# Fresh weight sums on VectorE for one pair of each gate quarter, and a fifth seven-product pair in the first

## The chip, the cores and the metric

The kernel runs on one core of a Trainium2 chip, in one launch. The metric is the device time of that launch in microseconds. All matrix products run on TensorE (PE); VectorE (DVE), ScalarE (ACT) and GpSimd (POOL) prepare operands and finish results; the queues of SyncE (SP), ScalarE and POOL start transfers, which share the core's 16 DMA engines.

## The reference

One encoder block, 256 tokens of width 2048, float32. What matters here is the middle of it, the two gates and what they multiply:

```python
h = rms_norm(x, attn_norm[i])
proj = h @ w_in[i]
qa, ka, va, qb, kb, vb, ga, gb = jnp.split(proj, split_points, axis=-1)
ya = windowed_gqa(qa, ka, va, rel_bias_table, sink_a[i])
yb = dilated_attention(qb, kb, vb, rel_bias_table)
merged = jax.nn.sigmoid(ga) * (ya @ w_branch_a[i]) + jax.nn.sigmoid(gb) * (yb @ w_branch_b[i])
x = x + merged @ w_out[i]
...
x = x + (jax.nn.gelu(g) * (hf @ w_ffn_up[i])) @ w_ffn_down[i]
gate_p = jax.nn.sigmoid(rms_norm(x, ple_norm[i]) @ w_ple_gate[i])
x = x + gate_p * (p[i] @ w_ple_proj[i])
```

`ga` and `gb` are each 2048 columns of `w_in`: 256 x 2048 by 2048 x 4096 in all.

## The kernel before

All weights lie in memory as one stream of pieces, 16 blocks of 128 x 128 each, in the order of use (`_stream`). A load brings half a piece (8 blocks, 512 KB) into one of six `raw` buffers. Every product is made to float32 accuracy from two parts: ScalarE copies the weights, rounded, to `whi` (L287), VectorE puts the rest, `raw - whi`, into `wlo` (L288), and three matmuls (`xhi*whi`, `xhi*wlo`, `xlo*whi`, L474 to L476) make one product. There are four `whi` and four `wlo` buffers, so a split can be at most four steps ahead of TensorE; a matmul of 512 columns follows the one before as soon as its operands are there.

The gates are made in four quarters (jobs `gab` 0 to 3). A quarter covers 4 blocks of columns of each gate and all 16 blocks of the inner dimension, taken as 8 pairs. Between the quarters stand the branch products (`ba`, `bb`, 8 and 4 blocks of the inner dimension). `seven_product` (L451) works a pair as a 2 x 2 by 2 x 2 block product, over the two inner blocks, the two halves of the tokens and the two gates: 8 products, or 7 by combining sums of operands as Strassen and Winograd do, after which VectorE and ScalarE combine the accumulators (`combined`). Which pairs take seven, and in which order the pairs come, is in `_pairs` (L141): in a quarter the order is 0, 4, 1, 2, 6, 3, 5, 7, and pairs 1, 2, 3 and 5 (`GATED`) take seven.

A pair by eight has two splits of 128 x 1024 and 24 matmuls. A pair by seven has four parts, with 3, 6, 6 and 6 matmuls, and `split_to` (L275) writes this order for VectorE: the `wlo` of part 0 (128 x 512); an add that makes the sum `t2` (L296); the `wlo` of part 1, the *sums* tile (128 x 1024); an add that makes `t4` (L298); the `wlo` of part 2 and of part 3, which reads both sums. `keep` holds this order fast. The sums tile of part 1 has two sums of weight blocks, b11 + b12 and b12 + b22. These are made ahead in memory: `sums_in_memory` (L327) has POOL copy two blocks within memory and add the others to them by accumulating transfers, at the places listed in `MADE_AT`, for the first `AHEAD` = 29 seven-pairs (5 of the values job `v8`, 16 of the gates, 8 of the output projection); later ones are made in another way (`quarters`). `back` (L351) loads the finished tile on SP's queue into one of two buffers, two pairs ahead.

The operand sums of the activations for a seven-pair (`of_input`) are made once, before. The first job that uses them, `v8`, takes five pairs by seven, 1, 2, 3, 5 and 6 (`FARS`, `of_first`); the sums for pair 6 lie in the tile `first`.

```python
GATED = (1, 2, 3, 5)
...
    if kind == "gab":
        return [0, 4, 1, 2, 6, 3, 5, 7], GATED
...
            if part == 0 and not _whole(a):
                keep(nc.vector.tensor_tensor(t2, raws[h][:, :4, :], pairs_of[a][:, :4, :], op=ALU.add))
            if part == 1:
                keep(nc.vector.tensor_tensor(t4, raws[h][:, 4:, :], t2, op=ALU.add))
```

Of the kernel before, what the change touches and what calls it, by code (L numbers as in the profile page):

```python
# [13 lines left out]
ALU = mybir.AluOpType  # L14
AX = mybir.AxisListType

P = 128
# [19 lines left out]
PIECE = 16  # L37
SUB = 8
# [21 lines left out]
def _plan():  # L60
# [48 lines left out]
    for half in range(2):  # L109
# [7 lines left out]
        for c in range(2):  # L117
# [5 lines left out]


TOGETHER = 3
AHEAD = 8 + 5 + 4 * 4
SAVED = 8
SPLIT = 4
ROWS = 7
# [3 lines left out]
GATED = (1, 2, 3, 5)  # L133
# [1 line left out]
FETCHED = ((24, 8), (28, 8), (32, 8), (36, 8), (38, 9), (38, 14), (49, 8), (49, 12))  # L135
MADE_AT = [(9, 1), (10, 8), (11, 14), (13, 4), (14, 12), (16, 14), (18, 2),
           (19, 4), (19, 9), (19, 14), (20, 8), (21, 3), (23, 8), (25, 8), (27, 12), (30, 0), (31, 14),
           (34, 0), (37, 0), (38, 4), (38, 11), (39, 2), (40, 6), (40, 12), (41, 3), (43, 4), (43, 11), (44, 5), (46, 0)]


def _pairs(kind, c):  # L141

    if kind == "pgs":
        return [0, 1, 4, 5, 2, 6, 7, 3], range(4, 8)
    if kind == "v8":
        return [0, 1, 2, 4, 3, 5, 6, 7], FARS
    if kind == "gab":
        return [0, 4, 1, 2, 6, 3, 5, 7], GATED
    if kind == "o":
        return ([2, 4, 5, 6, 7, 0, 1, 3] if c else [0, 1, 2, 4, 5, 6, 7, 3]), range(LATER, LATER + 4)  # L150
    if kind == "d1" and c == 1:
        return [5, 0, 1, 6, 2, 3, 7, 4, 8, 9, 10], range(5)
    return [8, 0, 1, 2, 3, 9, 4, 5, 6, 7, 10], range(SAVED)
# [32 lines left out]
_SEVEN, _EIGHT, _ENDS = [], set(), {}  # L186
# [5 lines left out]
def _whole(a):  # L192

    if _BLOCKS[a][0] == "w_in":
        return False
    return _BLOCKS[a][0] in ("w_out", "w_ple_gate") or (_BLOCKS[a + SUB][1] % FHALF) // 2 in WHOLE
# [19 lines left out]
def _encoder(ctx: ExitStack, tc, xt, pt, cols, table, onehot, mask, ident_in, last_gain, wts, xrows, out):  # L216
    nc = tc.nc
# [31 lines left out]
    keep = tc.keep_in_program_order  # L249


    raws, subs = {}, {}
    pairs_of, kept = {}, {}
# [21 lines left out]
    def split_to(i):  # L275
        while state["sub"] < min(i, len(_SUBS)):
            s = state["sub"]
            a, n, part = _SUBS[s]
            h, o = divmod(a, SUB)
            load_all(h + 6 + (part == 3))  # L280
            if part is None:
                src = raws[h][:, o:min(o + n, SUB), :]
            else:
                src = (raws[h + 1][:, :4, :], pairs_of.get(a), raws[h], raws[h + 1])[part]
            hi = wpool.tile(list(src.shape), FR, name="whi", bufs=4)
            lo = wpool.tile(list(src.shape), FR, name="wlo", bufs=4)
            nc.scalar.activation(hi, src, AF.Copy)  # L287
            ins = nc.vector.tensor_tensor(lo, src, hi.bitcast(F32), op=ALU.subtract)  # L288
            if a // PIECE * PIECE in _EIGHT:
                keep(ins)  # L290
            subs[s] = (hi, lo)
            state["sub"] = s + 1
            if part is not None:
                t2, t4 = raws[h + 1][:, 4:, :], raws[h + 1][:, :4, :]
            if part == 0 and not _whole(a):
                keep(nc.vector.tensor_tensor(t2, raws[h][:, :4, :], pairs_of[a][:, :4, :], op=ALU.add))  # L296
            if part == 1:
                keep(nc.vector.tensor_tensor(t4, raws[h][:, 4:, :], t2, op=ALU.add))  # L298
                j = _SEVEN.index(a)
                if all(not j <= e < j + (3 if j > _ENDS["gab"] else 2) for e in _LAST):  # L300
                    back()
# [49 lines left out]
    def back():  # L351

        j = state["back"]
        t = two_sums() if "ff" in held else ap_.tile([P, SUB, P], F32, name="sums", tag="near", bufs=2)
        pairs_of[_SEVEN[j]] = t
        nc.sync.dma_start(t, kept[j][0])
        state["back"] = j + 1

    def firsts_to(end):
# [226 lines left out]
    def at(i, f, *a):  # L586

        due.setdefault(i, []).append((f, a))
# [78 lines left out]
    b = ps.tile([NH, 2 * T], F32, name="misc")  # L667
# [232 lines left out]
    def of_input(m):  # L900
        e = SPLIT + 2 * GATED.index(m)
        return [shared[:, e + c, :].rearrange("p (b n) -> p b n", n=P) for c in range(2)]

    def of_first(m):
        if m in (2, 3, 5):
            return of_input(m)
        return [held["first"][:, 2 * (m == 6) + c, :].rearrange("p (b n) -> p b n", n=P) for c in range(2)]
# [215 lines left out]
    def fetch(t, c):  # L1123
# [8 lines left out]
    stills = {  # L1132
        "o": lambda k: held["merged"][k >= SPLIT][:, k - SPLIT * (k >= SPLIT), :], "ba": lambda k: yab[:, k, :],
        "bb": lambda k: yab[:, QH + k, :], "pp": lambda k: held["ps"][:, k, :], "pg": lambda k: held["pl"][:, k, :],
    }
    stills["v"] = movers["q"]

    for i, job in enumerate(_JOBS):
        kind, n, _, _, _, blocks = job
# [23 lines left out]

        for e, (j, k) in enumerate(MADE_AT):
            if j == i:
                at((j, k), sums_in_memory, e)
        if i == _FAR - 6:
            held["first"] = big.tile([P, SPLIT, 2 * T], FR, name="first", tag="b0", bufs=1)
            for j, m in ((0, 1), (1, 5), (2, 6), (4, 2), (5, 3)):
# [13 lines left out]
        if kind == "gg" or (kind == "g" and n == FHALF):  # L1183
            late = 3 * (kind == "g")
            for e in range(16 if kind == "gg" else 17):
                j = i + late + (9 * e // 4 if late else 5 * e // 2)
# [58 lines left out]
        elif kind in ("o", "d0", "d1", "gab", "pgs", "v8"):  # L1245
# [2 lines left out]
            tags = {a: b for e in range(2) for a, b in zip(names[e], places[e ^ {"gab": n != 3, "v8": 0}.get(kind, n)])}  # L1248
            if (kind, n) == ("gab", 0):
                tags.update(p3="sp", p4="sp", c22="acc", p1="acc", p6="pt", p7="pt", p5="misc")  # L1250
            still, sums_at = {"o": (stills["o"], early), "gab": (stills["v"], of_input), "pgs": (stills["pg"], of_residual),
                               "v8": (stills["v"], of_first)}.get(
                kind, (lambda k: held["act"][:, k, :], shl))
            if kind == "v8":
# [134 lines left out]
```

## Time and profile before

| | us |
|---|---|
| median of three runs | 1443.81 (1443.23 to 1443.97) |
| the profiled execution | 1444.3 |
| its span, first to last instruction | 1442.5 |
| first gate quarter (`gab` 0) on TensorE | 312.9 to 356.3 |
| second, third, fourth | 361.7 to 403.5, 419.8 to 461.5, 461.5 to 502.3 |
| granted TensorE clock, mean | 0.998 |

A row of the timeline gives the start in us, how long the instructions took in us, the engine, the line, the operation, output <- inputs by the program's names, sizes and a count; in brackets stands the idle time of the engine ahead of it, and what ended that. Neighbours of one kind are merged into a row (x2), which then runs from the first one's start to the last one's end; on VectorE and ScalarE an instruction starts a little before the last one's end. Matmuls overlap: the spacing of their starts is what one costs, not the length shown.

### The profile page before, as it was taken

Reading aid. Unit: us, or ns where it says so; the run is one execution under the profiler, and the core shown is the slowest. Engines: PE = TensorE matmul, PEld = TensorE weight load, DVE = VectorE, ACT = ScalarE, POOL = GpSimd, SP = SyncE. Lnnn points to the kernel's source line nnn. Section 1 sums busy time; section 2 is a strip of 40 time slices with the busy share of each in tenths; the row PEclk is TensorE's granted clock in tenths of the full one; section 3 lists DMA queues with packets and bytes.
Section 4 is the critical chain, followed back from the end, with each engine's and each line's share of the span. In section 5 each row is a group of like instructions: output and inputs, shape, how many; then the busy total and the mean of one; then the engine's idle time right before and its main releaser. Section 6 shows DMA issues by size and latency. Waiting matters only on the chain.

```text
span 1442.5 us, 21000 instructions
## 1 busy us (share of the span) xinstructions
PE 1431.2 (99%) x7452; PEld 1227.1 (85%) x7452; DVE 1183.9 (82%) x1635; ACT 876.3 (61%) x1256; POOL 188.3 (13%) x291
## 2 busy tenths in 40 slices
PE   9999999999999999999999999999999999999997
PEld 8898888888888888888888888888888888888886
DVE  7798966668879878878888878997888887998896
ACT  7576654456656656775555556776555555677864
POOL 0022222111222110201111100102111110010000
PEclk9999999999999999999999999999999999999999
DMA  9798998889999978968888887989988888799672
GB/s 327 252 244 255 301 292 247 253 231 295 293 295 320 279 238 301 300 220 301 301 287 296 288 300 243 266 292 299 310 307 303 314 302 295 250 294 285 211 240 93
DMA packets 128149, 397.31 MB, mean 275 GB/s; under 512 B 14628, under 2 KB 19876, under 8 KB 127916
## 3 DMA queue, kind: packets, MB, share of 16 engines
q1 hardware_dynamic: 93372, 300.79, 60.4%
q0 software_dynamic: 32656, 91.24, 24.4%
q10 hardware_dynamic: 2016, 3.94, 0.9%
q8 instruction: 58, 0.95, 0.3%
q14 instruction: 47, 0.39, 0.1%
HBM read 363.11 MB, written 58.76 MB: 292 GB/s over the span
## 4 chain that ended last, share of the span: by engine, by line
PE 95%; DVE 2%; DMA 1%; ACT 1%; issue 0%; SPq 0%; POOLq 0%; DVEq 0%; ACTq 0%
PE acc L395 29%; PE acc L398 15%; PE acc L475 12%; PE acc L476 12%; PE acc L474 12%; PE acc L423 3%; PE acc L425 3%; PE acc L424 3%; PE first L372 2%; DMA raw<-in_wts 1%; DVE wlo L288 1%; PE pt L987 1%; PE pt L754 1%; PE acc L447 0%; ACT whi L287 0%
## 5 line engine op out<-in xcount | busy, mean ns | idle before, releaser
L288 DVE TENSOR_TENSOR wlo<-raw,whi 128x1024 fp32r<-128x1024 f32 (+2 forms) x581 | 660.8, 1158 | 94.9 <-ACT whi L287 87.2
L287 ACT ACTIVATE whi<-raw 128x1024 fp32r<-128x1024 f32 (+2 forms) x581 | 573.5, 1005 | 234.6 <-PE acc L476 92.0
L395 PE MATMUL acc<-mov,whi 128*128 128x512 f32 x1840 | 441.3, 391 | 0.0
L395 PEld LDWEIGHTS acc<-mov,whi 128*128 128x128 f32 x1840 | 337.8, 188 | 65.5
L398 PEld LDWEIGHTS acc<-mov,wlo 128*128 128x128 f32 x1840 | 237.3, 191 | 9.0 <-ACT mov L531 0.2
L398 PE MATMUL acc<-mov,wlo 128*128 128x256 f32 x1840 | 243.1, 283 | 0.0
L512 ACT ACTIVATE t<-acc 128x256 f32<-128x256 f32 x115 | 43.6, 379 | 149.6 <-PE acc L395 149.6
L476 PE MATMUL acc<-whi,mov 128*128 128x512 f32 x259 | 100.8, 389 | 0.0
L475 PE MATMUL acc<-wlo,mov 128*128 128x512 f32 x259 | 100.8, 389 | 0.0
L474 PE MATMUL acc<-whi,mov 128*128 128x512 f32 x259 | 100.6, 390 | 0.0
L288 DVE TENSOR_TENSOR wlo<-sums,whi 128x1024 fp32r<-128x1024 f32 x62 | 75.5, 1219 | 8.9 <-ACT whi L287 8.9
L474 PE MATMUL acc<-whi,act 128*128 128x512 f32 x207 | 80.9, 391 | 0.0
L475 PE MATMUL acc<-wlo,act 128*128 128x512 f32 x207 | 80.7, 390 | 0.0
L476 PE MATMUL acc<-whi,act 128*128 128x512 f32 x207 | 80.7, 390 | 0.0
L287 ACT ACTIVATE whi<-sums 128x1024 fp32r<-128x1024 f32 x62 | 65.4, 1056 | 20.4 <-PE acc L476 9.4
L934 POOL DMA_DIRECT2D x<-row x33 | 28.5, 908 | 310.8 <-PE acc L476 106.0
L325 POOL DMA_DIRECT2D kept<-sums x33 | 17.8, 540 | 360.2 <-DVE sums L321 219.4
L475 PE MATMUL acc<-wlo,merged 128*128 128x512 f32 x164 | 64.1, 391 | 0.3 <-DVE wlo L288 0.2
L474 PE MATMUL acc<-whi,merged 128*128 128x512 f32 x164 | 64.0, 390 | 0.0
L476 PE MATMUL acc<-whi,merged 128*128 128x512 f32 x164 | 63.9, 389 | 0.0
L857 ACT ACTIVATE c<-c 128x256 f32<-128x256 f32 x44 | 18.3, 417 | 67.2 <-DVE c L855 67.2
L476 PEld LDWEIGHTS acc<-whi,mov 128*128 128x128 f32 x259 | 48.6, 188 | 10.1
(274 smaller groups left out, 2147.9 us busy)
## 6 DMA issues: line engine op xcount, KB each, us to landing
raw<-in_wts SPq DMA_DIRECT2D x452, 512.0 KB, 6.0
sums<-kept SPq DMA_DIRECT2D x62, 512.0 KB, 5.8
kept<-in_wts POOLq DMA_DIRECT2D x66, 256.0 KB, 8.0
sums<-in_wts POOLq DMA_DIRECT2D x33, 512.0 KB, 7.3
kept<-sums POOLq DMA_DIRECT2D x33, 512.0 KB, 4.6
raw<-in_wts SPq DMA_DIRECT2D x64, 256.0 KB, 5.2
kept<-in_wts POOLq DMA_DIRECT2D x29, 512.0 KB, 7.7
x<-row POOLq DMA_DIRECT2D x33, 256.0 KB, 7.9
```

The source lines that it names most:

```text
L287: nc.scalar.activation(hi, src, AF.Copy)
L288: ins = nc.vector.tensor_tensor(lo, src, hi.bitcast(F32), op=ALU.subtract)
L372: nc.tensor.matmul(firsts[e][:, T * low:], w, m[:, :2 * T - T * low], start=(k == 0 and not low), stop=(k == KC - 1 and low != turned), sk ...
L395: nc.tensor.matmul(acc, hi[:, k, :], m, start=(first and k == 0), stop=(last and k == SUB - 1), skip_group_check=True)
L398: nc.tensor.matmul(acc[:, T:], lo[:, k, :], m[:, :T], start=False, stop=False, skip_group_check=True)
L423: nc.tensor.matmul(acc, xh, hi, start=(k == 0), stop=False)
L424: nc.tensor.matmul(acc, xh, lo, start=False, stop=False)
L425: nc.tensor.matmul(acc, xl, hi, start=False, stop=(k == n - 1 - t * late))
L474: nc.tensor.matmul(acc, xh, hi, start=(e == 1), stop=False)
L475: nc.tensor.matmul(acc, xh, lo, start=False, stop=False)
L476: nc.tensor.matmul(acc, xl, hi, start=False, stop=(e == uses[name]))
L512: keep(nc.scalar.activation(t, acc[:, T:], AF.Copy, scale=scale))
```

## The change

For one pair of each quarter, number 8, 13, 17 and 21 in the list of all seven-pairs (`FRESH`), the sums of weights aren't made in memory. `back` loads the two blocks as they are, b11 and b12, and VectorE makes both sums in place where they are used, by two adds of 128 x 512 behind the `wlo` of part 0. Number 8 is pair 6 of the first quarter, which took eight products before and now takes seven, with the operand sums in `first`; the order there becomes 0, 4, 1, 2, 3, 6, 5, 7. Numbers 13, 17 and 21 are pair 5, the last seven-pair, of the other quarters. `sums_in_memory` is run for 26 pairs instead of 29, and `MADE_AT` moves the last ones.

```diff
 TOGETHER = 3
-AHEAD = 8 + 5 + 4 * 4
+AHEAD = 5 + 5 + 3 * 4 + 8
...
-           (34, 0), (37, 0), (38, 4), (38, 11), (39, 2), (40, 6), (40, 12), (41, 3), (43, 4), (43, 11), (44, 5), (46, 0)]
+           (34, 0), (36, 8), (37, 6), (38, 5), (38, 12), (41, 3), (43, 6), (45, 2), (46, 2)]
+FRESH = (8, 13, 17, 21)
+KEPT = [j for j in range(AHEAD) if j not in FRESH]
...
+    if kind == "gab" and c == 0:
+        return [0, 4, 1, 2, 3, 6, 5, 7], (*GATED, 6)
     if kind == "gab":
         return [0, 4, 1, 2, 6, 3, 5, 7], GATED
...
+            if part == 0 and _SEVEN.index(a) in FRESH:
+                two, b22 = pairs_of[a], raws[h][:, :4, :]
+                for dst, more in ((two[:, :4, :], two[:, 4:, :]), (two[:, 4:, :], b22)):
+                    keep(nc.vector.tensor_tensor(dst, dst, more, op=ALU.add))
             if part == 0 and not _whole(a):
...
-        nc.sync.dma_start(t, kept[j][0])
+        nc.sync.dma_start(t, wts[_SEVEN[j] // PIECE].rearrange("p (b n) -> p b n", n=P)[:, SUB:, :] if j in FRESH else kept[j][0])
...
+    def of_gated(m):
+        return of_first(m) if m == 6 else of_input(m)
...
-                at((j, k), sums_in_memory, e)
+                at((j, k), sums_in_memory, KEPT[e])
...
-            still, sums_at = {"o": (stills["o"], early), "gab": (stills["v"], of_input), "pgs": (stills["pg"], of_residual),
+            still, sums_at = {"o": (stills["o"], early), "gab": (stills["v"], of_gated), "pgs": (stills["pg"], of_residual),
```

VectorE's queue at the last seven-pair of the second quarter (pair 5). Before, from part 0 to part 3 and the first split of pair 7; `raw_3999` and `raw_3990` are the pair's loaded blocks, `sums_3962` its sums tile:

```order
L288 TENSOR_TENSOR wlo_4083<-raw_3999,whi_4082 128x512
L296 TENSOR_TENSOR raw_3999<-raw_3990,sums_3962 128x512
L288 TENSOR_TENSOR wlo_4094<-sums_3962,whi_4093 128x1024
L298 TENSOR_TENSOR raw_3999<-raw_3990,raw_3999 128x512
L288 TENSOR_TENSOR wlo_4107<-raw_3990,whi_4106 128x1024
L288 TENSOR_TENSOR wlo_4128<-raw_3999,whi_4127 128x1024
L288 TENSOR_TENSOR wlo_4137<-raw_4011,whi_4136 128x1024
```

Now, the same place (the lines L288, L296 and L298 have become L292, L304 and L306, and the tiles are `raw_4010`, `raw_4001` and `sums_3982`):

```order
L292 TENSOR_TENSOR wlo_4094<-raw_4010,whi_4093 128x512
L302 TENSOR_TENSOR sums_3982<-sums_3982 128x512
L302 TENSOR_TENSOR sums_3982<-sums_3982,raw_4001 128x512
L304 TENSOR_TENSOR raw_4010<-raw_4001,sums_3982 128x512
L292 TENSOR_TENSOR wlo_4107<-sums_3982,whi_4106 128x1024
L306 TENSOR_TENSOR raw_4010<-raw_4001,raw_4010 128x512
L292 TENSOR_TENSOR wlo_4120<-raw_4001,whi_4119 128x1024
L292 TENSOR_TENSOR wlo_4132<-raw_4010,whi_4131 128x1024
L292 TENSOR_TENSOR wlo_4141<-raw_4022,whi_4140 128x1024
```

Two adds stand between the split of part 0 and all the rest of the pair, and the split of the sums reads what they write.

VectorE's queue in the first quarter, from the last split of pair 2. Before, pair 6 follows with two splits (`raw_3410`, `raw_3434`), then pair 3:

```order
L288 TENSOR_TENSOR wlo_3561<-raw_3404,whi_3560 128x1024
L288 TENSOR_TENSOR wlo_3570<-raw_3410,whi_3569 128x1024
L288 TENSOR_TENSOR wlo_3582<-raw_3434,whi_3581 128x1024
L288 TENSOR_TENSOR wlo_3594<-raw_3519,whi_3593 128x512
L296 TENSOR_TENSOR raw_3519<-raw_3509,sums_3485 128x512
```

Now pair 3 (`raw_3446`, `raw_3422`, `sums_3497`) follows at once, and then pair 6, of which part 0 and the adds are shown:

```order
L292 TENSOR_TENSOR wlo_3576<-raw_3416,whi_3575 128x1024
L292 TENSOR_TENSOR wlo_3585<-raw_3446,whi_3584 128x512
L304 TENSOR_TENSOR raw_3446<-raw_3422,sums_3497 128x512
L292 TENSOR_TENSOR wlo_3596<-sums_3497,whi_3595 128x1024
L306 TENSOR_TENSOR raw_3446<-raw_3422,raw_3446 128x512
L292 TENSOR_TENSOR wlo_3609<-raw_3422,whi_3608 128x1024
L292 TENSOR_TENSOR wlo_3621<-raw_3446,whi_3620 128x1024
L292 TENSOR_TENSOR wlo_3630<-raw_3525,whi_3629 128x512
L302 TENSOR_TENSOR sums_3554<-sums_3554 128x512
L302 TENSOR_TENSOR sums_3554<-sums_3554,raw_3515 128x512
L304 TENSOR_TENSOR raw_3525<-raw_3515,sums_3554 128x512
```

The pair with two splits, which stood between two and two seven-pairs, is gone from there; five seven-pairs follow one another, and the fourth has the adds.

## The prediction

> **What bounds the kernel now.** I read the page's busy shares and its chain of waits first, then the four gate quarters as windows, then TensorE's, VectorE's and ScalarE's timelines inside one quarter.
>
> ```profile
> span 1442.5 us, 21000 instructions
> PE 1431.2 (99%) x7452; PEld 1227.1 (85%) x7452; DVE 1183.9 (82%) x1635; ACT 876.3 (61%) x1256; POOL 188.3 (13%) x291
> PE 95%; DVE 2%; DMA 1%; ACT 1%; issue 0%; SPq 0%; POOLq 0%; DVEq 0%; ACTq 0%
> ```
> TensorE is busy for 99% of the span and holds 95% of the chain. So whatever TensorE has to wait for adds to the time one for one, and a matmul that is dropped shortens it by one issue interval. The windows below are the four gate quarters (columns: time, busy us of PE, PEld, DVE, ACT, POOL with counts, granted clock, DMA share, GB/s).
>
> ```profile
> 312.80:356.30 43.50, 43.19 (x198) 35.40 (x196) 34.11 (x38) 24.98 (x32) 6.09 (x8) 1.00 0.88 286
> 361.70:403.45 41.75, 41.75 (x189) 34.62 (x189) 37.21 (x44) 24.34 (x31) 9.40 (x15) 1.00 0.99 296
> 419.70:461.50 41.80, 41.80 (x191) 34.66 (x190) 36.35 (x42) 23.46 (x28) 8.68 (x14) 1.00 0.97 298
> 461.50:502.30 40.80, 40.80 (x182) 33.79 (x181) 35.66 (x42) 27.40 (x32) 6.14 (x9) 1.00 0.95 275
> ```
> In the quarters TensorE is full, VectorE has 4 to 6 us free in each, the DMA engines almost nothing, and POOL is mostly idle. Whether VectorE's free time is where the new adds go is what the timelines must tell. This is the last seven-product pair of the second quarter (pair 5, behind pair 3), TensorE first: the first matmul and the one behind it of each of the four parts, and the start of the next pair.
>
> ```profile
> 393.25 0.39 PE L474 MATMUL acc<-whi,mov 128*128 128x512 f32 x1
> ...
> 393.93 0.39 PE L474 MATMUL acc<-whi,merged 128*128 128x512 f32 x1
> 394.16 0.39 PE L475 MATMUL acc<-wlo,merged 128*128 128x512 f32 x1
> ...
> 395.29 0.39 PE L474 MATMUL acc<-whi,merged 128*128 128x512 f32 x1
> 395.52 0.39 PE L475 MATMUL acc<-wlo,merged 128*128 128x512 f32 x1
> ...
> 396.65 0.39 PE L474 MATMUL acc<-whi,mov 128*128 128x512 f32 x1
> 396.88 0.39 PE L475 MATMUL acc<-wlo,mov 128*128 128x512 f32 x1
> ...
> 398.01 0.39 PE L474 MATMUL acc<-whi,mov 128*128 128x512 f32 x1
> ```
> From 393.25 to 398.01 are 21 matmuls: 4.76 us, one each 0.227 us. Every part needs its whi at the first of the two times and its wlo at the second. VectorE in the same stretch (the first row is the last split of pair 3 and part 0 of pair 5), and then ScalarE:
>
> ```profile
> 389.83 1.83 DVE L288 TENSOR_TENSOR wlo<-raw,whi 128x1024 fp32r<-128x1024 f32 x2 [1.54 <-ACT whi L287]
> 391.58 0.68 DVE L296 TENSOR_TENSOR raw<-raw,sums 128x512 f32<-128x512 f32 x1
> 392.18 1.22 DVE L288 TENSOR_TENSOR wlo<-sums,whi 128x1024 fp32r<-128x1024 f32 x1
> 393.32 0.68 DVE L298 TENSOR_TENSOR raw<-raw 128x512 f32<-128x512 f32 x1
> 393.92 1.22 DVE L288 TENSOR_TENSOR wlo<-raw,whi 128x1024 fp32r<-128x1024 f32 x1
> 395.21 1.23 DVE L288 TENSOR_TENSOR wlo<-raw,whi 128x1024 fp32r<-128x1024 f32 x1
> ```
> ```profile
> 390.78 1.06 ACT L287 ACTIVATE whi<-sums 128x1024 fp32r<-128x1024 f32 x1 [0.46 <-ACT whi L287]
> 394.12 2.01 ACT L287 ACTIVATE whi<-raw 128x1024 fp32r<-128x1024 f32 x2 [0.87 <-PE acc L476]
> ```
> VectorE is never idle from 389.83 to 395.14, and its margins are thin: the wlo of the sums ends at 393.40 and is wanted at 394.16 (0.76 us); part 2's ends at 395.14, wanted at 395.52 (0.38); part 3's at 396.44, wanted at 396.88 (0.44). The 1.54 us of idle time stand ahead of the pair, where VectorE waits for a whi and the whi for a free buffer (four of them, given back by TensorE). Lead can't be saved up beyond that ring.
>
> **The change part by part.** *The matmuls.* Pair 6 of the first quarter becomes 21 matmuls instead of 24: 3 x 0.227 = **-0.68 us**, and TensorE is full there, so it counts.
>
> *The adds in quarters two to four.* Each last pair gets two adds of 128x512 behind the wlo of its part 0, and the whi of the sums has to wait for both. The trace has such a pair of adds elsewhere (L321), and a ScalarE split released by a VectorE add:
>
> ```profile
> 711.04 0.69 DVE L321 TENSOR_TENSOR sums<-sums 128x512 f32<-128x512 f32 x1
> 711.76 0.69 DVE L321 TENSOR_TENSOR sums<-row,sums 128x512 f32<-128x512 f32 x1
> ```
> ```profile
> 346.37 0.69 DVE L298 TENSOR_TENSOR raw<-raw 128x512 f32<-128x512 f32 x1
> ```
> ```profile
> 347.17 2.01 ACT L287 ACTIVATE whi<-raw 128x1024 fp32r<-128x1024 f32 x2 [1.19 <-DVE raw L298]
> ```
> So the second add starts 0.72 behind the first and takes 0.69, and ScalarE starts 0.11 after an add's end (347.17 less 347.06). On VectorE, starts lie 0.60 apart behind a 512 piece and 1.14 behind a 1024 piece (391.58 to 392.18 to 393.32). Step by step, from 391.58:
> - The adds run 391.58 to 392.27 and 392.30 to 392.99, the third add (old L296) from 392.90.
> - The whi of the sums runs 393.10 to 394.16; before it ran 390.78 to 391.84. TensorE wants it at 393.93 and is some 0.3 late.
> - Its wlo starts at 394.20 (0.04 behind the whi, as 395.21 stands behind 394.12 + 1.06) and ends at 395.42: 1.3 behind the 394.16 when it is wanted.
> - The L298 add starts at 395.34, part 2's wlo runs 395.94 to 397.16: some 1.7 behind 395.52, counting 0.05 from its end to the matmul.
> - Part 3's whi waits for the L298 add (396.02 + 0.11) and ends at 397.19, its wlo at 398.45: 1.6 behind 396.88, no further loss.
>
> The waits lie on one chain, so the last and largest stands for all: 1.7, and up to 0.1 more for a first matmul that takes longer behind a wait (0.34 instead of 0.23 in the rows below). I take **1.75 us**, three times: **+5.25**. Bounds: not under 0.56 a quarter (the adds' 1.32 less the margin of 0.76, if ScalarE's wait cost nothing), not over 1.8. The rows carry the waits too, so I stay near the upper end. The other quarters' margins are in the same place with the same distances, since their order on VectorE is the same.
>
> *The first quarter.* The order was 0, 4, 1, 2, 6, 3, 5, 7 with 1, 2, 3, 5 by seven; now 1, 2, 3, 6, 5 follow one another, all by seven, with the adds in 6. VectorE spends 3 x 0.60 + 3 x 1.14 = 5.2 us on such a pair and TensorE 4.76, so each one in a row loses 0.46; pair 6 by eight (24 matmuls, 5.44 us, two splits, 2.3 us) had made that good. Up to the end of pair 2 nothing changes:
>
> ```profile
> 332.20 2.36 DVE L288 TENSOR_TENSOR wlo<-raw,whi 128x1024 fp32r<-128x1024 f32 x2
> ```
> ```profile
> 333.87 0.39 PE L475 MATMUL acc<-wlo,mov 128*128 128x512 f32 x1
> ...
> 335.01 0.39 PE L474 MATMUL acc<-whi,mov 128*128 128x512 f32 x1
> ```
> The last wlo of pair 2 (the first of the two in that row) ends at 332.20 + 1.22 = 333.42, 0.45 ahead of its matmul, and the next pair starts on TensorE at 335.01. With the same steps as above, pair 3's wlos end at 334.02, 335.76, 337.50 and 338.79: 0.3 late at part 2. Pair 6: part 0 ends at 339.39, adds to 340.72, whi of the sums 340.83 to 341.89, its wlo to 343.15, L298 to 343.75, part 2's wlo to 344.89, wanted at 342.04: 2.9 late. Pair 5 loses another 0.6: part 2's wlo ends at 350.26, wanted at 346.80. In all **+3.6** with the slower restart. Pair 7 by eight follows and gives the lead back.
>
> This quarter has a wait already, at pair 5 (TensorE), behind a late load (queue of SP, then ScalarE):
>
> ```profile
> 345.89 0.39 PE L474 MATMUL acc<-whi,merged 128*128 128x512 f32 x1
> 346.51 0.50 PE L475 MATMUL acc<-wlo,merged 128*128 128x512 f32 x1 [0.24 <-DVE wlo L288]
> 346.85 0.39 PE L476 MATMUL acc<-whi,merged 128*128 128x512 f32 x1
> ...
> 347.77 0.40 PE L474 MATMUL acc<-whi,merged 128*128 128x512 f32 x1
> 348.25 0.50 PE L475 MATMUL acc<-wlo,merged 128*128 128x512 f32 x1
> ```
> ```profile
> 332.16 1.62 SPq L264 DMA_DIRECT2D raw<-in_wts  x2
> ```
> ```profile
> 343.36 0.63 ACT L287 ACTIVATE whi<-raw 128x512 fp32r<-128x512 f32 x1 [1.61 <-DMA raw<-in_wts]
> ```
> The gaps of 0.62, 0.34 and 0.48 (and 0.33 behind that) exceed 0.227 by 0.87 in all. In the new chain part 0 of pair 5 isn't due on ScalarE before about 344.7, so a load that lands at 343.36 again holds nothing up: **-0.87**.
>
> *The sums in memory.* Three steps fewer (26 for 29), each a 1-element instruction on ScalarE and POOL and three to five POOL transfers. POOL waits for nothing that TensorE needs, so they are worth nothing directly; they take transfers from DMA engines that are 0.95 to 0.99 busy in quarters two to four. The fresh sums are one SP transfer of the same 512 KB in the same place of SP's queue, now without POOL's work ahead of it. Nothing is queued behind a new wait on SP. On ScalarE the other splits stand behind the delayed whi; they are in the chain above. The later steps of the list start a little later than before, but serve pairs of the output projection, after 524 us: nothing.
>
> *Sum:* 5.25 + 3.6 - 0.87 - 0.68 = **+7.3 us**. The profiled execution took 1444.3 (span 1442.5 and 1.8 around it), which gives 1451.6; it was 0.5 above the median 1443.81, so I forecast **1451.1 us**.
>
> The Trainium skill, "Perfetto Trace Analysis", section "Identifying the Most-Contended Engine", takes occupancy as the measure for VectorE and says to optimize the engine with the highest share. By it, VectorE at 82% under a TensorE at 99% would have room for the adds, and only the three matmuls would show: the first rival below. The windows agree on the share, the timeline doesn't on the room.
>
> **The rivals.**
> - *Not slower: the adds fall into VectorE's idle time.* For it: 4.5 to 5.5 us free in each of quarters two to four, adds of 1.3 us. Then TensorE's work decides: -0.68, or -1.55 with the old wait gone: 1442.3 to 1443.1. It holds if the whi of the sums gets done within 0.76 us of its old margin. Against it: the idle time is ahead of the pair, the adds stand behind part 0. Chance 0.08.
> - *Five in a row cost nothing* since ScalarE and VectorE get further ahead in pairs 0 and 4 than I see; only the late quarters pay, and the first keeps its old wait: 5.25 - 0.68 = +4.6, 1448.4. Against it: the ring of four and the margin of 0.45 at 333.42. Chance 0.08.
> - *Loads become late in the first quarter.* More is loaded in less time there, and a load issued at about 333.5 landed at 343.36, 9.9 us later. The fresh sums can be asked for at 330.4 and are due at 339.3: at 9.9 us they come 1.0 late, and pair 5's behind them about as much: +1 to +3, some 1453. Chance 0.12.
>
> **How the numbers follow.** The forecast has 0.72, and its own range is 1449.4 to 1452.8. The low end of 1447.0 takes in the second rival and late quarters at 1.2 us; the high end of 1453.4 most of the third. Outside stay the first rival and a few hundredths. About 0.2%, 2.9 us, is what a measurement of this kernel can tell from no change: over 1446.7 lie the forecast and two rivals, 0.90 with a little taken off for mis-sized waits; within it the first rival, 0.09; under 1440.9 nothing that I can name, 0.01.
>
> **What would show it.** In the new trace: TensorE gaps behind the second matmul of the sums in the last pair of quarters two to four, 1.6 to 1.8 us in each; VectorE's two new adds directly behind a 512 split and ScalarE's sums split 0.1 behind them; in the first quarter small gaps in pair 3, over 2 us in pair 6, half a us in pair 5. It would be wrong if the gaps there stay under 0.5 us, if the sums split starts ahead of the adds' end, or if the gaps are ended by a DMA.

## The result and the profile after

The changed kernel takes **1453.39 us** (median of four runs, 1452.94 to 1457.94) against 1443.74 for the kernel before on the same chip, 9.65 us more. The ratio of the two medians is 1.0067; estimated over all the runs it is 1.0073, 95% interval 1.006 to 1.0085. That is slower, as forecast. The forecast was 1451.1 with a range up to 1453.4. The median lies at the very end of that range, 1.0073 times 1443.81 would be 1454.4, and two later measurements of the same kernel gave 1453.27 and 1453.93. So some 2.3 us of the 9.2 to 9.9 are not in the forecast's sum, and the question is where they come from.

The page of the changed kernel, first the span and the busy shares, then the chain of waits by engine (the profiled execution took 1457.94, the longest of the four):

```profile
span 1456.2 us, 20998 instructions
PE 1436.2 (99%) x7449; PEld 1225.1 (84%) x7449; DVE 1192.5 (82%) x1647; ACT 877.2 (60%) x1255; POOL 177.7 (12%) x279
PE 90%; DVE 4%; DMA 3%; ACT 2%; issue 1%; SPq 0%; ACTq 0%; POOLq 0%; DVEq 0%
```

The busy shares say nothing: TensorE 99% and VectorE 82%, as before. The chain says it: TensorE holds 90% where it held 95%, and VectorE and the DMA engines have gained two points each. The same four quarters as windows (columns as before the change):

```profile
312.80:361.00 48.20, 45.51 (x198) 34.61 (x196) 36.72 (x42) 25.01 (x32) 9.37 (x15) 1.00 0.98 305
367.00:411.00 44.00, 41.17 (x181) 32.46 (x180) 40.11 (x48) 27.22 (x32) 0.81 (x1) 1.00 0.69 215
427.50:471.00 43.50, 42.70 (x190) 34.49 (x189) 36.29 (x42) 23.82 (x29) 5.08 (x7) 1.00 0.82 247
471.00:513.50 42.50, 41.72 (x182) 33.59 (x181) 37.04 (x43) 26.00 (x30) 0.00 (x0) 1.00 0.63 207
```

Each is longer than TensorE is busy in it. And POOL has moved: 15 records in the first quarter instead of 8, one in the second instead of 15. What TensorE waits for, from the view of waits (waited for, us in total, times, longest):

```profile
PE acc L482 <- ACT whi L291: 4.6, 12, 1.6
PE acc L483 <- DVE wlo L292: 2.0, 3, 1.1
PE acc L482 <- DVE th L1312: 1.4, 1, 1.4
...
PE acc L431 <- DVE th L925: 0.7, 1, 0.7
```

The first two are the splits. The last two are of another kind: there TensorE waits for an accumulator that VectorE has not emptied yet.

**The last pair of a quarter** lost what was forecast, by the forecast's chain but at other matmuls. Pair 5 of the second quarter, timeline of TensorE, then of VectorE, then of ScalarE:

```profile
401.30 0.39 PE L484 MATMUL acc<-whi,mov 128*128 128x512 f32 x1
401.87 0.73 PE L482 MATMUL acc<-whi,merged 128*128 128x512 f32 x2 [0.18 <-ACT whi L291]
402.81 0.50 PE L482 MATMUL acc<-whi,merged 128*128 128x512 f32 x1 [0.21 <-ACT whi L291]
...
404.07 0.40 PE L484 MATMUL acc<-whi,merged 128*128 128x512 f32 x1
404.88 0.50 PE L482 MATMUL acc<-whi,mov 128*128 128x512 f32 x1 [0.41 <-ACT whi L291]
```
```profile
399.17 0.69 DVE L302 TENSOR_TENSOR sums<-sums 128x512 f32<-128x512 f32 x1
399.89 0.69 DVE L302 TENSOR_TENSOR sums<-sums,raw 128x512 f32<-128x512 f32 x1
400.50 0.69 DVE L304 TENSOR_TENSOR raw<-raw,sums 128x512 f32<-128x512 f32 x1
401.85 1.23 DVE L292 TENSOR_TENSOR wlo<-sums,whi 128x1024 fp32r<-128x1024 f32 x1 [0.66 <-ACT whi L291]
402.99 0.69 DVE L306 TENSOR_TENSOR raw<-raw 128x512 f32<-128x512 f32 x1
```
```profile
400.75 1.06 ACT L291 ACTIVATE whi<-sums 128x1024 fp32r<-128x1024 f32 x1 [2.84 <-DVE sums L302]
401.72 1.04 ACT L291 ACTIVATE whi<-raw 128x1024 fp32r<-128x1024 f32 x1
...
403.77 2.96 ACT L291 ACTIVATE whi<-raw 128x1024 fp32r<-128x1024 f32 x3 [0.52 <-DVE raw L306]
```

The second add ends at 400.58, the split starts 0.17 later and ends at 401.81, the matmul behind it starts at 401.87 instead of 401.53 (401.30 + 0.227). The rest follows from that: the whi of part 2 stands behind this split on ScalarE and ends at 402.76 (the matmul at 402.81); the wlo waits 0.66 us, the L306 add stands behind the wlo and ends at 403.68, and the whi of part 3 behind the add (403.77 to 404.83; the matmul at 404.88, where 404.30 was due).

**A place that the forecast held to cost nothing** is the stretch behind the first quarter, 356 to 376 us, the branch product and the start of the next quarter. ScalarE, then VectorE, then TensorE:

```profile
358.75 1.06 ACT L291 ACTIVATE whi<-raw 128x1024 fp32r<-128x1024 f32 x1 [3.67 <-DMA raw<-in_wts]
363.03 1.06 ACT L291 ACTIVATE whi<-raw 128x1024 fp32r<-128x1024 f32 x1 [3.23 <-DMA raw<-in_wts]
```
```profile
359.84 1.22 DVE L292 TENSOR_TENSOR wlo<-raw,whi 128x1024 fp32r<-128x1024 f32 x1 [2.34 <-ACT whi L291]
360.98 0.68 DVE L925 TENSOR_TENSOR th<-acc,th 128x512 f32<-128x512 f32 x1
364.12 1.22 DVE L292 TENSOR_TENSOR wlo<-raw,whi 128x1024 fp32r<-128x1024 f32 x1 [2.46 <-ACT whi L291]
...
366.46 1.88 DVE L1312 TENSOR_TENSOR th<-acc,th 128x512 f32<-128x512 f32 x3
...
368.86 0.69 DVE L1312 TENSOR_TENSOR th<-acc,th 128x512 f32<-128x512 f32 x1
```
```profile
361.72 0.50 PE L431 MATMUL acc<-whi,yab 128*128 128x512 f32 x1 [0.72 <-DVE th L925]
...
369.60 0.50 PE L482 MATMUL acc<-whi,mov 128*128 128x512 f32 x1 [1.40 <-DVE th L1312]
...
374.87 0.50 PE L483 MATMUL acc<-wlo,mov 128*128 128x512 f32 x1 [0.63 <-DVE wlo L292]
```

Read it from the bottom up. TensorE waits at 361.72 and 369.60 for steps that empty accumulators (L925, which ends at 361.66, and the last L1312, which ends at 369.55); at 374.87 it waits for a weight split that stands behind more of them. VectorE works in a fixed order, and these steps stand there behind two weight splits that wait 2.34 and 2.46 us for ScalarE, which waits 3.67 and 3.23 us for weights. None of these splits or steps was changed. The trace of before has no wait of TensorE here.

### The profile page after: what moved, and what is told of

The parts are those of the page before. It is cut to its first block, busy times and chain, and to the rows that moved or that the text cites. A ratio compares the mean times of both kernels' runs of the same rounds, so it can differ in the third digit from the quotient of the medians.

```text
span 1456.2 us, 20998 instructions
## 1 busy us (share of the span) xinstructions
PE 1436.2 (99%) x7449; PEld 1225.1 (84%) x7449; DVE 1192.5 (82%) x1647; ACT 877.2 (60%) x1255; POOL 177.7 (12%) x279
## 4 chain that ended last, share of the span: by engine, by line
PE 90%; DVE 4%; DMA 3%; ACT 2%; issue 1%; SPq 0%; ACTq 0%; POOLq 0%; DVEq 0%
PE acc L403 29%; PE acc L406 15%; PE acc L483 10%; PE acc L484 10%; PE acc L482 10%; PE acc L431 3%; PE acc L432 3%; PE acc L433 3%; PE first L380 2%; DVE wlo L292 2%; ACT whi L291 1%; DMA raw<-in_wts 1%; DMA sums<-kept 1%; DMA sums<-in_wts 1%; PE pt L998 1%
## 5 line engine op out<-in xcount | busy, mean ns | idle before, releaser
L292 DVE TENSOR_TENSOR wlo<-raw,whi 128x1024 fp32r<-128x1024 f32 (+2 forms) x582 | 661.9, 1159 | 91.8 <-ACT whi L291 84.2
L482 PE MATMUL acc<-whi,mov 128*128 128x512 f32 x254 | 99.3, 393 | 3.1 <-ACT whi L291 1.7
L483 PE MATMUL acc<-wlo,mov 128*128 128x512 f32 x254 | 99.2, 390 | 1.8 <-DVE wlo L292 1.8
L484 PE MATMUL acc<-whi,mov 128*128 128x512 f32 x254 | 98.9, 390 | 0.0
L292 DVE TENSOR_TENSOR wlo<-sums,whi 128x1024 fp32r<-128x1024 f32 x63 | 76.9, 1221 | 10.8 <-ACT whi L291 10.8
L482 PE MATMUL acc<-whi,act 128*128 128x512 f32 x207 | 80.8, 390 | 0.0
L483 PE MATMUL acc<-wlo,act 128*128 128x512 f32 x207 | 80.7, 390 | 0.0
L483 PE MATMUL acc<-wlo,merged 128*128 128x512 f32 x164 | 64.7, 395 | 0.5 <-DVE wlo L292 0.2
L482 PE MATMUL acc<-whi,merged 128*128 128x512 f32 x164 | 63.9, 395 | 1.2 <-ACT whi L291 1.2
L482 PEld LDWEIGHTS acc<-whi,mov 128*128 128x128 f32 x254 | 47.7, 188 | 14.8 <-ACT whi L291 3.4
```

The lines of the kernel that those rows point to most:

```text
L482: nc.tensor.matmul(acc, xh, hi, start=(e == 1), stop=False)
L483: nc.tensor.matmul(acc, xh, lo, start=False, stop=False)
L484: nc.tensor.matmul(acc, xl, hi, start=False, stop=(e == uses[name]))
```

## The experiments

Theory A is the forecast with one addition: late pairs 5 us, first quarter some 2 us net, and the rest from weight loads that come late because POOL's steps now stand in the first quarter. Each diff is against the changed kernel. Columns: median; how far it is above the median of the kernel before that was run beside it (1443.74 to 1444.04), with the interval of the ratio; and TensorE's gaps over 0.3 us, each a spacing of two starts less the usual 0.227 us, added up in the first quarter, from there to 380 us, and in the last pair of quarters two, three and four. The gaps are those of the one profiled execution, whose time can lie off the median: the first row's took 1457.94 us, that of again 1452.28.

| kernel | us | above | ratio | first | to 380 | last pairs |
|---|---|---|---|---|---|---|
| the change | 1453.39 | 9.65 | 1.006 to 1.0085 | 3.1 | 3.3 | 1.3, 1.3, 1.3 |
| again | 1453.27 | 9.23 | 1.0057 to 1.0082 | 2.5 | 0.8 | 1.3, 1.3, 1.3 |
| again2 | 1453.93 | 9.91 | 1.0054 to 1.008 | 2.6 | 1.9 | 1.3, 1.3, 1.3 |
| late_only | 1449.99 | 5.95 | 1.0031 to 1.0056 | 0 | 0 | 1.3, 1.4, 1.3 |
| late_only2 | 1449.11 | 5.09 | 1.0023 to 1.0048 | 0 | 0 | 1.3, 2.0, 1.3 |
| first_only | 1446.33 | 2.29 | 1.0008 to 1.0026 | 2.6 | 0 | 0, 0, 0 |
| first_kept | 1444.71 | 0.67 | 0.9996 to 1.0014 | 0.4 | 0 | 0, 0, 0 |
| pool_later | 1451.88 | 7.90 | 1.0041 to 1.0066 | 2.5 | 0 | 1.3, 1.3, 1.3 |
| pool_later2 | 1450.67 | 6.65 | 1.0032 to 1.0059 | 2.5 | 0 | 1.3, 1.3, 1.3 |
| adds_ahead | 1451.37 | 7.39 | 1.0037 to 1.0064 | 2.3 | 1.8 | 0.5, 0.5, 0.5 |
| fresh_first | 1450.13 | 6.15 | 1.0028 to 1.0053 | 0.4 | 3.1 | 0, 0, 0 |
| spread | 1445.85 | 1.87 | 1.0009 to 1.0026 | 2.0 | 0 | 0, 0, 0 |
| quiet | 1443.64 | -0.38 | 0.9986 to 1.0004 | 0 | 0 | 0, 0, 0 |

Smaller gaps come on top: with them a late pair's quarter has 1.6 to 1.7 us (the matmuls behind a wait take 0.33 apart), and the first quarter of first_only 3.5, that of first_kept 1.3 and that of adds_ahead 5.2, where it is 0.95 in the kernel before.

**The change twice more** (again, again2), unedited.

> The changed kernel once more, for a second trace of it. Measured so far: 1453.4 us, with one execution of four at 1457.9, and that one was profiled. Theory A (waits in the gate quarters make the loss): 1453, with TensorE gaps of 1.6 us in the last pair of each of quarters two to four, some 4 to 5 us inside the first quarter and 2 to 4 us behind it; the gap of 1.3 us at 1364.8 of the first trace is chance and is missing. Rival: the whole excess of the profiled execution is a part of the change, and the gap at 1364.8 is there again.

> The changed kernel a third time. Theory A (what is lost behind the first quarter comes from loads that POOL's steps in that quarter make late): the median stays at 1452.3 to 1453.8, TensorE has over 2 us of gaps between 361 and 380 us, and splits there wait for weight loads that took over 10 us. Rival (chance in two profiled executions): no gaps over 0.3 us between 361 and 380.

Both medians agree with the first. The gaps up to 380 us are there each time but differ in size, 3.3, 0.8 and 1.9 us, as the loads come more or less late. The expectations of over 2 us there, and of 4 to 5 us inside the first quarter, were too high. The gap near 1365 us of the first profile is not there again.

**One half of the change each** (late_only, first_only), and the first quarter's order without its adds (first_kept: five by seven in a row, the sums of all five from memory). POOL's steps stand at the places of before, less three in late_only and with one more in first_kept. The edit of late_only, without the lines on `AHEAD` and `MADE_AT` (12, 16 and 20 are pair 5 of quarters two to four again, counted with one seven-pair fewer):

```diff
-FRESH = (8, 13, 17, 21)
+FRESH = (12, 16, 20)
...
-    if kind == "gab" and c == 0:
-        return [0, 4, 1, 2, 3, 6, 5, 7], (*GATED, 6)
```

first_only has this, and first_kept an empty list in its place:

```diff
-FRESH = (8, 13, 17, 21)
+FRESH = (8,)
```

> Fresh sums in the last pair of quarters two to four alone; the first quarter and the list of the steps in memory as before, less the three. Theory A (ScalarE's split of the sums waits for the two adds): three gaps of 1.6 us, 4.9 us in all, 1448.6 us. Rival (VectorE's idle time takes the adds, and the loss belongs to the first quarter): 1443.7 to 1444.5.

> The first quarter alone with its fifth pair and fresh sums there; the list of the steps in memory at before's places. Theory A (the chain of five pairs and the adds costs 3.6 inside the quarter, the old wait of 0.87 and three matmuls go; the waits behind the quarter come from POOL's moved steps): +2.1, 1445.8 us, and no waits behind the quarter. Rival B (five pairs in a row give the load buffers back so late that the loads behind the quarter are late whatever POOL does): +4.5 to +5, 1448.5 us, with gaps behind the quarter.

> The first quarter with its fifth pair, but all sums made in memory (30 steps; the additional one where POOL is free, in the job 22); no fresh sums anywhere. Theory A: five in a row cost 1.5 us (0.46 a pair and slower restarts), less 0.68 and 0.87: 1443.7 us, nothing behind the quarter. Rival B (late buffers): gaps behind the quarter, 1445 to 1446.5.

> Fresh sums for the last seven-pair of quarters two to four alone, a second time; the first profile had a gap of 1.59 us at 1357 us, at a gain load of 6.7 us. If that is chance from execution to execution: 1449.0 to 1450.0, the gain load at 4.7 to 5.3 us in the profiled execution and no such gap, so that three times 1.63 us is all that is left over before. If the changed kernel makes that load late: again 6.4 us or more and a gap over 1.2.

The late pairs cost 5.1 to 6.0 us; three times 1.63 are 4.9. The first profile of late_only has one more gap, of 1.59 us near the end, behind a gain load that is there 6.7 us after its issue; the second has none, so it is no part of the edit. The second has 0.7 us more in the third quarter instead, where ScalarE waits 1.19 us for a weight load, and it lacks the old wait of the first quarter. The first quarter costs 2.3 us net, with its gaps at the sums, and nothing behind it. Five by seven in a row with sums from memory cost 1.3 us in gaps, which the three matmuls and the old wait pay back: net, nothing that this measurement can tell. So the two halves together make 7.4 to 8.2 (the lower sum is some 0.9 too low, as both its parts gain the old wait, which can be gained but once), and the change makes 9.2 to 9.9: 1 to 2 us come only when both are there, which is when the list of POOL's steps moves. The intervals are 1.3 to 1.8 us wide to each side, so the sums alone don't prove it; the traces say more, since neither half has a gap over 0.3 us behind the first quarter.

**POOL's steps out of the first quarter** (pool_later, pool_later2). With fewer steps in the list, those at (37, 6), (38, 5) and (38, 12) are now steps for the output projection, which have five transfers where those of the gates have three. Here the three stand at places behind the quarter. (The second expectation says two; it is the same kernel, with three entries moved.)

```diff
-           (34, 0), (36, 8), (37, 6), (38, 5), (38, 12), (41, 3), (43, 6), (45, 2), (46, 2)]
+           (34, 0), (36, 8), (39, 2), (40, 6), (40, 12), (41, 3), (43, 6), (45, 2), (46, 2)]
```

> The changed kernel with three of POOL's steps in memory taken out of the first quarter and put behind it: (37, 6), (38, 5), (38, 12) become (39, 2), (40, 6), (40, 12), where before had steps too. Theory A (two separate changes, quarters two to four +4.9 and the first +2.3, and the rest of the loss is loads made late by these steps): 1451.1 us, no gaps from 355 to 375 us. Rival C (the loads behind the first quarter are late because VectorE and ScalarE give the buffers back late when both parts of the change are there): 1453.3 us as the changed kernel, with those gaps.

> The changed kernel with two of POOL's steps of the first quarter moved behind it, a second time. Theory A: 1451.1 to 1452.2, 1 to 2 us under the changed kernel of the same call, no gap over 0.3 us between 356 and 380 us, and the loads issued there land within 8 us. Rival: within 0.5 us of the changed kernel.

The time falls to 1451.88 and 1450.67, on both sides of the forecast (the second is under its expected range), and the gaps behind the first quarter are gone. pool_later2 ran beside again2: 3.3 us apart in the medians, and each of its five executions (1450.26 to 1451.95) is faster than each of again2's (1452.87 to 1454.36). POOL's timeline in the changed kernel (one of its three steps in the quarter), then in pool_later2, where the row's bracket tells that it did nothing for 53 us:

```profile
329.96 0.56 POOL L344 DMA_DIRECT2D kept<-in_wts  x1
330.51 0.55 POOL L347 DMA_DIRECT2D kept<-in_wts  x1
339.45 0.83 POOL L348 DMA_DIRECT2D kept<-in_wts  x1 [8.39 <-DMA kept<-in_wts]
340.00 1.17 POOL L349 DMA_DIRECT2D kept<-in_wts  x1
347.89 0.82 POOL L351 DMA_DIRECT2D kept<-kept  x1 [6.72 <-DMA kept<-in_wts]
```
```profile
363.81 0.19 POOL L337 TENSOR_TENSOR edges<-edges,mhalf 128x1 f32<-128x1 f32 x1 [53.48 <-ACT edges L336]
```

And what this does to the five weight loads that the late splits wait for: the DMA view of six microseconds, changed kernel (352 to 358 us), then pool_later2 (349.5 to 355.5 us, the same loads). Queue q0 is POOL's, q1 SP's; the last row has the median time from issue to landing.

```profile
q0 software_dynamic: 278, 0.78, 49.4%
q1 hardware_dynamic: 241, 0.88, 40.8%
...
raw<-in_wts SPq DMA_DIRECT2D x5, 512.0 KB, 10.8
```
```profile
q1 hardware_dynamic: 462, 1.69, 80.8%
...
raw<-in_wts SPq DMA_DIRECT2D x5, 512.0 KB, 6.1
```

The same loads take 10.8 us with POOL's transfers beside them and 6.1 without, and SP's queue moves 0.88 MB in six microseconds instead of 1.69: about half. The Trainium skill, "DMA: Bandwidth & Descriptors", section "Queues, rings and completion order", says that each DMA engine goes round the queues that have work, a packet from each in turn. The shares here agree with it: packets of the two queues took 49.4% and 40.8% of the engines' time, though SP had five loads waiting. Without POOL the split there waits for TensorE to give back a buffer, not for DMA; ScalarE in pool_later2:

```profile
357.97 1.06 ACT L289 ACTIVATE whi<-raw 128x1024 fp32r<-128x1024 f32 x1 [1.66 <-PE acc L482]
```

The executions in order of what these five loads took (four of them in fresh_first; the last column is the table's "to 380"):

| kernel | median of the five loads, us | share of the engines' time in q0's packets | gaps from the first quarter's end to 380 us |
|---|---|---|---|
| pool_later, pool_later2 | 6.1, 6.1 | none | 0, 0 |
| first_only | 7.8 | 23% | 0 |
| before | 7.9 | 13% | 0 |
| again | 8.2 | 39% | 0.8 |
| again2 | 9.2 | 50% | 1.9 |
| the change | 10.8 | 49% | 3.3 |
| fresh_first | 11.1 | 41% | 3.1 |

The loss begins where the loads take some 8 us, and it is larger where they take longer. first_only and before have steps of POOL in the quarter too, but two, with three transfers each.

**The place of the adds.** adds_ahead has the two adds ahead of the wlo of part 0 instead of behind it. fresh_first keeps all but the pair: the fresh sums are those of the first seven-pair (pair 1) of each quarter instead of the last (in the first quarter, instead of pair 6). spread has these pairs too, the order 0, 1, 2, 4, 3, 6, 5, 7 in the first quarter, the loads of sums asked for earlier, and POOL's steps moved as in pool_later.

In adds_ahead the four lines of the diff that begin with `if part == 0 and _SEVEN.index(a) in FRESH` stand some lines further up, ahead of the `wlo`. The edit of fresh_first is its one line on `FRESH`; spread has the other two as well:

```diff
-FRESH = (8, 13, 17, 21)
+FRESH = (5, 10, 14, 18)
...
-        return [0, 4, 1, 2, 3, 6, 5, 7], (*GATED, 6)
+        return [0, 1, 2, 4, 3, 6, 5, 7], (*GATED, 6)
...
-                at((i, 1 + 2 * e), back)
+                at((i, e), back)
```

> The changed kernel with the two adds ahead of the split of part 0 instead of behind it: same work on VectorE, but ScalarE's split of the sums can start 0.6 us earlier. Theory A (the chain adds, ScalarE's split, VectorE's split, add, split): the loss of a late quarter falls from 1.63 to some 1.1 us (0.7 at the split of the sums, 1.1 at part 2) and that of pair 6 by as much, 1451.3 us in all. Rival D (only the 1.3 us of added work on VectorE counts, wherever it stands in the pair): gaps as in the changed kernel, 1453.3 us.

> The changed kernel with the fresh sums in the first seven-pair of each quarter (pair 1, behind two pairs by eight) instead of pair 6 and the last ones; the same number of adds and of steps in memory, the same five in a row in the first quarter. Theory A (what costs is that the adds stand where the split of the sums has 0.76 us of margin; at pair 1 it has over 3): no gaps in quarters two to four, 1.5 us in the first for five in a row, 1443.9 us, and up to 1445.5 with late loads behind the first quarter. Rival D (added work on VectorE counts wherever it stands): 1450 to 1453.

> As fresh_first, with the first quarter in the order 0, 1, 2, 4, 3, 6, 5, 7, so that at most three pairs by seven stand in a row, its first two sums tiles asked for one and two steps earlier, and POOL's three steps behind the first quarter as in pool_later. Theory A: the third in a row loses 0.3 to 0.4, three matmuls fewer give 0.7, the old wait of 0.87 may go: 1443.0 to 1443.7 us, a little faster than before. Rival: pair 1 comes before the lead is built up, and gaps stand at its adds: 1445 or more.

With the adds ahead, a late pair loses 0.5 us in gaps over 0.3 instead of 1.3, and 1.0 to 1.1 instead of 1.6 to 1.7 with the small ones, as expected. In the first quarter, where as much was to be gained, that order is worse in the profiled execution (the longest of five, 1453.34): 5.2 us with the small gaps, against 3.4 in again. So it was partly luck that the median came out at the expected 1451.3. The two blocks land late there, the adds wait for them, and now the wlo of part 0 waits behind the adds. VectorE, then TensorE:

```profile
341.16 0.69 DVE L292 TENSOR_TENSOR sums<-sums 128x512 f32<-128x512 f32 x1 [1.82 <-DMA sums<-in_wts]
```
```profile
343.23 0.55 PE L483 MATMUL acc<-wlo,mov 128*128 128x512 f32 x1 [2.09 <-DVE wlo L296]
```

fresh_first came out 4.6 us above the range that theory A gave it. Quarters two to four have no gap over 0.3 us, with the same adds (one of 0.26 is in the second). The largest loss left is the place behind the first quarter, 3.1 us, the same waits as in the changed kernel with no fresh pair at the end of the quarter. POOL's steps are in its first quarter as in the changed kernel. Another 2.4 us are in the first quarter, most of them in gaps under 0.3, and about 1 us stands before the gates (161 to 164 us). ScalarE, then TensorE:

```profile
355.11 1.06 ACT L291 ACTIVATE whi<-raw 128x1024 fp32r<-128x1024 f32 x1 [3.00 <-DMA raw<-in_wts]
```
```profile
360.66 0.50 PE L431 MATMUL acc<-whi,yab 128*128 128x512 f32 x1 [1.56 <-DVE th L925]
```

spread has nothing there, as POOL's steps are gone, but it loses 2 us at pair 1 of the first quarter, where the blocks for the sums come late (the first add waits 3.37 us for them). Its rival, 1445 or more, was right.

**A version without either loss** (quiet): fresh sums for pair 1 of quarters two to four, the first quarter's order and sums as before, and none of POOL's steps in it. It makes the same 26 sums in memory as the change and three of its four fresh pairs.

```diff
-AHEAD = 5 + 5 + 3 * 4 + 8
+AHEAD = 5 + 4 * 4 + 8
-           (34, 0), (36, 8), (37, 6), (38, 5), (38, 12), (41, 3), (43, 6), (45, 2), (46, 2)]
-FRESH = (8, 13, 17, 21)
+           (34, 0), (39, 2), (40, 6), (40, 12), (41, 3), (43, 4), (43, 11), (44, 5), (46, 0)]
+FRESH = (9, 13, 17)
-    if kind == "gab" and c == 0:
-        return [0, 4, 1, 2, 3, 6, 5, 7], (*GATED, 6)
```

> Fresh sums for the first seven-pair (pair 1) of quarters two to four, the first quarter worked as before with its sums from memory, and none of POOL's steps (37, 0), (38, 4), (38, 11) in it: 26 sums in memory and six VectorE adds, as three quarters of the change have. Theory A (the place of the adds costs, not their number): no gap over 0.2 us in quarters two to four, the old wait of 0.87 us in the first quarter smaller or gone, 1442.9 to 1444.0. Rival (VectorE has no room for the adds in a quarter at all): 1448 or more, with over 1 us of gaps in each of the three quarters.

1443.64 against 1444.02, an interval from 0.9986 to 1.0004: no difference that can be measured, and the rival (no room for the adds in a quarter at all) is out. The old wait of 0.87 us in the first quarter is gone in the trace, and quarters two to four have one gap over 0.2, of 0.24 us (479 us). Pair 1 of the second quarter, VectorE, ScalarE, and the first matmul of the sums on TensorE:

```profile
366.55 0.69 DVE L298 TENSOR_TENSOR sums<-sums 128x512 f32<-128x512 f32 x1
367.27 0.69 DVE L298 TENSOR_TENSOR sums<-sums,raw 128x512 f32<-128x512 f32 x1
...
369.17 1.23 DVE L288 TENSOR_TENSOR wlo<-sums,whi 128x1024 fp32r<-128x1024 f32 x1 [0.61 <-ACT whi L287]
```
```profile
368.08 1.06 ACT L287 ACTIVATE whi<-sums 128x1024 fp32r<-128x1024 f32 x1 [3.66 <-DVE sums L298]
```
```profile
373.29 0.39 PE L478 MATMUL acc<-whi,merged 128*128 128x512 f32 x1
373.52 0.39 PE L479 MATMUL acc<-wlo,merged 128*128 128x512 f32 x1
```

The chain is the same, with the same wait of the wlo. But the wlo of the sums ends at 370.40 and is wanted at 373.52: 3.1 us early, after the adds, where the last pair had 0.76 us before them. Two pairs by eight stand ahead of pair 1, with two splits each for 24 matmuls, and they give the lead.

## Why the forecast fell short

- **The matmuls, -0.68.** Three fewer (7449 for 7452), as said. No run has them alone.
- **Late quarters, +5.25.** Right: 1.63 each where 1.75 was taken, 4.9 in all in the gaps, 5.1 and 6.0 in the two measurements. The forecast had the waits end with a wlo. The three largest waits all end with a whi: in the changed program several matmuls with a whi (L482) stand ahead of the first with the new wlo (L483, 403.38 us), so the wlo is no longer what comes last. The chain is the same.
- **First quarter, +3.6 less 0.87 and 0.68, so some +2.1.** Right: first_only measured 2.3. Inside it the adds count for more than the five in a row: first_only has 3.5 us of gaps there, first_kept, without the adds, 1.3. So the second rival was wrong in its reason, since five in a row do cost; but what they save, the old wait and three matmuls, is as much, and first_kept is only 0.67 above before, not told from nothing.
- **The step that failed: "The later steps of the list start a little later than before, but serve pairs of the output projection, after 524 us: nothing."** They do not start later: the first such step stood at 362.3 us in the trace of before and stands at 291.9 in the first profile of the change. And the nothing asked when their results are due, not what their transfers share. The list is three entries shorter, so five-transfer steps now stand in the first quarter: of the 15 records of POOL there, 12 are transfers, where 6 of 8 were. Beside them the weight loads take 8.2 to 10.8 us, without them 6.1, and splits behind the quarter wait. Behind these stand the steps that empty TensorE's accumulators. Measured: 3.3 us side by side (again2's 9.91 above before, less pool_later2's 6.65), 1.3 from one measurement to another (again's 9.23 less pool_later's 7.90), and 0.8, 1.9 and 3.3 us in the gaps of three executions. With these three entries moved, the sum of the other terms, 7.3, stands: 6.65 and 7.90 were measured.
- **The third rival** (loads late in the first quarter, some 1453) had the time and the cause, loads, but another place. VectorE did wait 0.47 us for the blocks of the fresh sums in the first profile (341.20 us), where the quarter has 1.7 us more of gaps than in again. The most was lost behind the quarter, and to POOL's queue rather than to the extra loading: first_only loads the same weights for five by seven and loses nothing there.
- **The first rival** (the adds fall into VectorE's idle time) was false for this place and true for another. (VectorE's free time ahead of the change was 9.4 us in the first quarter, not 4 to 6 as in the others; nothing in the sum rests on it.) The Trainium skill, "Perfetto Trace Analysis", section "Identifying the Most-Contended Engine", takes occupancy as the measure for VectorE. In quiet VectorE is busy for 37.04 of 41.8 us of the third quarter and nothing waits; in the changed kernel for 36.29 of 43.5, and TensorE loses 1.6. So the reading of it that stands behind this rival, that a share of 82% leaves room for adds, does not hold here: the lead at the place of the adds tells, not the share.

What stays open: why the same loads take 8.2 us in one execution of the changed kernel and 10.8 in another, and whether the number of POOL's transfers, their bytes or their place counts most. No run changed one of these alone.

## What to carry to other kernels

Before work is put on an engine with idle time, measure at the very place how far its result is ahead of its use: 1.3 us of adds cost 1.6 where the lead was 0.76, and nothing where over 3 us were left after them. When a list of background work gets shorter, look at what now stands in the old places; its transfers share the DMA engines with the weights, whatever their own due time. And follow a late load through the fixed order of the engine behind it: in the first trace, what TensorE waited for at the two longest gaps was not the late split but a step queued behind it.

## What the runs showed of the hardware

- Two kernels moved about the same bytes in six microseconds at the loads behind the first quarter, 1.92 MB each, but five loads of 512 KB took 10.8 us beside POOL's queue and 6.1 alone. The rate does not tell which queue gets it.
- A matmul of 512 columns starts 0.227 us after the one before; the one behind a wait lets the next start 0.33 to 0.34 after it (404.88 to 405.22 in the trace of the change). So three waits of 1.3 us in all cost 1.6.
- One load of 1 MB near the end (the last gain) took 4.8 us in one execution of the changed kernel and 6.4 in another, with a gap of 1.3 us on TensorE (1365 us). VectorE in again2 waits 1.71 us for it, in the first profile 3.15. A wait of 1.5 to 1.9 us stands in the other profiles, before's too, and costs TensorE nothing; only in two, at 3.15 and 3.46 (late_only), does TensorE have a gap, and it belongs to no edit.

```profile
1357.62 1.23 DVE L1239 TENSOR_SCALAR end<-end 128x2048 f32<-128x2048 f32 x1 [1.71 <-DMA end<-in_last_gain]
```
```profile
1361.66 1.23 DVE L1239 TENSOR_SCALAR end<-end 128x2048 f32<-128x2048 f32 x1 [3.15 <-DMA end<-in_last_gain]
```
